# Turning the rotated q with VectorE squares and a buffer in HBM instead of with TensorE

## The chip, the core and the metric

One core of a Trainium2 chip runs the whole layer. The metric is the device time of one execution in microseconds (us), the median of several runs. Beside the runs there is one profiled execution: every engine's instructions with their times, the DMAs and the clock granted to TensorE.

## What is computed

The reference is one layer of a decoder trunk on 256 positions of width 1024: a SwiGLU feed-forward half-step, a mixer of two attentions, a second half-step and a final norm. The change lies in the mixer, in the first attention ("MoBA"):

```python
proj = u @ w_in
q_a, k_a, v_a, q_b, k_b, v_b, g_a, g_b = jnp.split(proj, cuts, axis=-1)
q_a = partial_rotary(split_heads(q_a, N_HEADS_MOBA), positions)
k_a = partial_rotary(split_heads(k_a, N_HEADS_MOBA), positions)
y_a = merge_heads(moba_attention(q_a, k_a, split_heads(v_a, N_HEADS_MOBA)))
```

There are 8 heads of 64. The rotation changes the first 16 numbers of each head's 64. With 256 positions there is one block of keys, so this attention is a causal softmax of q·k.

## The kernel before

Positions stand on the 128 partitions, in two halves t = 0 and 1. A matrix product takes tiles of 128 rows by 512 columns of weights. Each number is split into a high and a low part, so that one product of a tile is three matmuls (`mm3`, L290; one call of `unit`, L296, is one half with one tile).

**Weights.** `Weights` (L129) loads tiles in pairs: `raw74` is load 74 and holds the tiles 148 and 149. Three load buffers take turns, so that load n+3 waits until both tiles of load n have been read by VectorE. ScalarE casts the high part (`wh`, L163), VectorE the low one (`wl`, L164); ten buffers of each take turns, and `pump` runs up to seven tiles ahead of TensorE. Tiles 132 to 139 are those of q, 140 to 147 of k, 148 to 155 of v.

**Order.** TensorE and SyncE run what the program writes, in that order; in this stretch the other engines do too. Side work is put between the units by `Weave`: a piece of work is a generator, `tick` is called once for a unit, and `yield n` lets n units pass. The constants at the top (`D_TURN`, `D_LANDED` and so on) are such counts.

**Projection and heads.** `project` (L648) does the 16 units of one projection: all eight tiles of t = 0 and then those of t = 1 for q, t = 1 two tiles behind t = 0 after that. Results are taken out of three accumulator banks by ScalarE (`evac`, L678). `rotate` (L660) is four instructions on POOL. `turn` (L692) then brings q and k from positions on the partitions to heads on the partitions, which the scores need: here by eight TensorE transposes of 128x128 into two PSUM banks (`qtpa`, `ktpa`, L701). ScalarE casts the high part (`qTha`, L313) and VectorE makes the low part (`qTla`, L314), in two halves of 512 columns each. The second attention's q and k are not rotated and go another way: VectorE transposes squares of 32x32 (L689), and sixteen DMAs from SBUF to SBUF let the squares change places (`exchange`, L413).

**The use.** `moba_pair` (L765) makes the scores `S` of two heads, adds the mask, makes the softmax on ScalarE and VectorE, transposes it on TensorE (`ptp`, L794) and multiplies with v. The first pair starts when q and k are there.

Of the kernel before, what the change touches and what calls it, by code (L numbers as in the profile page):

```python
# [8 lines left out]
F32 = mybir.dt.float32  # L9
# [8 lines left out]
P = 128  # L18
# [19 lines left out]
D_TURNED = 3  # L38
# [3 lines left out]
D_PIECE = 2  # L42
D_TURN = 10
D_READY = 7
D_NORM = 4
D_SQUARES = 3
D_EIGHT = 6
# [141 lines left out]
def hybrid_layer_kernel(ctx, tc, x, xt, pos, g_final, bgate, wstream, out):  # L189
    nc = tc.nc  # L190
# [3 lines left out]
    ordered.enter_context(tc.manual_schedule())  # L194
    consts = ctx.enter_context(tc.tile_pool(name="consts", bufs=1))
    wpool = ctx.enter_context(tc.tile_pool(name="wpool", bufs=1))
    work = ctx.enter_context(tc.tile_pool(name="work", bufs=1))
    psum = ctx.enter_context(tc.tile_pool(name="psum", bufs=1, space=PSUM))

# [9 lines left out]
    def big(nm, dt=F32R):  # L209
        return work.tile([P, 1024], dt, name=nm, tag="big", bufs=24)  # L210
# [7 lines left out]
    def row512(nm):  # L218
        return work.tile([P, 512], F32, name=nm, tag="tok", bufs=4)
# [66 lines left out]
    weave = Weave()  # L286
# [30 lines left out]
    def square(t, ms, cols):  # L317
        junk = work.tile([P, D], BF16, name=f"sq_{ms.name}", tag="junk", bufs=1)
        nc.scalar.activation(junk[:, cols], h[t][:, cols], AF.Square, scale=1.0 / 32.0, accum_out=ms)
# [55 lines left out]
    class Given(Normed):  # L375
# [15 lines left out]
        def blk(self, k):  # L391
            o = k % 4 * T + self.t * P
            return [q[:, o:o + P] for q in self.made[k // 4 * 2:k // 4 * 2 + 2]]

    def lagged(n, lag):

        for k in range(n + lag):
            if k < n:
                yield 0, k
            if k >= lag:  # L400
                yield 1, k - lag
# [4 lines left out]
    def slots(q, n):  # L406

        return q[:, 0:n * P].rearrange("p (g s w) -> p s g w", g=4, s=n)

    def plain(q):  # L410
        return q.rearrange("p (s g w) -> p s g w", g=4, w=32)

    def exchange(moved, squares, n, queues, gap):  # L413

        w = 32
        for m in range(16):
            i, j = divmod(m, 4)
            queues[m % len(queues)].dma_start(moved[j * w:j * w + w, i * n * w:(i + 1) * n * w],
                                              squares[i * w:i * w + w, j * n * w:(j + 1) * n * w])
            if m % len(queues) == len(queues) - 1:  # L420
                yield gap


    def ffn(base, xn, nm, on_half, lag, last=False):

# [2 lines left out]
        squares = {}  # L428

        def hidden(b, t, bank):  # L430
# [10 lines left out]
            nc.vector.transpose(dst, plain(sh[:, 256:512]))  # L441
            if t == 1 and (b % 2 or b == FB - 1):
                weave.add(turn_hidden(p, n), D_TURNED)

        def later(f, *args):
            f(*args)
            return
            yield

        def turn_hidden(p, n):  # L450
            moved = big(f"hm_{nm}{p}", F32)
            yield from exchange(moved, squares[p], n, [nc.sync], D_MOVE)
            yield D_MOVED
            hts[p] = big(f"hth_{nm}{p}"), big(f"htl_{nm}{p}")
            split(plain(hts[p][0][:, 0:n * P]), plain(hts[p][1][:, 0:n * P]), slots(moved, n))

        for b in range(FB):
# [14 lines left out]
            for t, k in lagged(KD, 2 if b else lag) if b or lag else ():  # L472
                if k == 0:
                    banks[t] = acc_bank(f"gu_{nm}{b}_{t}")
                i = base + b * KD + k
# [53 lines left out]
        for t, c in ((0, 0), (0, 1), (1, 0), (1, 1)) if last else ((0, 0), (1, 0), (0, 1), (1, 1)):  # L529
            pieces = (0, 1) if last and (t, c) == (1, 1) else (None,)  # L530
            for piece in pieces:
                for k in range(head, KF):
                    i = base + 2 * head + c * tail + k - head
# [91 lines left out]
    def next_norm(dst, nm):  # L625
        def on_half(t, c, piece=None):
# [9 lines left out]
            else:  # L636
                weave.add(go(), D_NORM)

# [21 lines left out]
    def rotate(dst, t):  # L660

        d3 = dst.rearrange("p (h d) -> p h d", d=HD)
        t1 = work.tile([P, NH, 16], F32, name=f"t1_{dst.name}", tag="rot1", bufs=2)
        t2 = work.tile([P, NH, 16], F32, name=f"t2_{dst.name}", tag="rot2", bufs=2)
        g = nc.gpsimd
        g.tensor_mul(t1, d3[:, :, 0:16], cos[:, t, :].unsqueeze(1).to_broadcast([P, NH, 16]))
        g.tensor_mul(t2[:, :, 0:8], d3[:, :, 8:16], sin[:, t, 0:8].unsqueeze(1).to_broadcast([P, NH, 8]))
        g.tensor_mul(t2[:, :, 8:16], d3[:, :, 0:8], sin[:, t, 8:16].unsqueeze(1).to_broadcast([P, NH, 8]))
        marks["rot"] = g.tensor_add(d3[:, :, 0:16], t1, t2).ins

    def heads(b0, nm, res, rotary, diagonal):


        for j, which in enumerate("qk"):
            src = {}
            squares = None if rotary else big(f"{which}s{nm}", F32)

            def evac(t, ps, j=j, which=which, src=src, squares=squares):  # L678
                dst = row512(f"{which}{nm}{t}")
                if j == 0:  # L680
                    if nm == "a":
                        nc.gpsimd.tensor_scalar(rq[t], un[t].r, 0.125, None, op0=ALU.mult)
                    nc.scalar.activation(dst, ps, AF.Copy, scale=rq[t])
                else:
                    nc.scalar.activation(dst, ps, AF.Copy, scale=un[t].r)
                if rotary:
                    rotate(dst, t)
                else:
                    nc.vector.transpose(slots(squares, 8)[:, t:t + 7:2], plain(dst))  # L689
                src[t] = dst  # L690

            def turn(which=which, src=src, squares=squares):  # L692
                if rotary:
                    tp = two_banks(f"{which}tp{nm}")
                else:
                    tp = big(f"{which}m{nm}", F32)
                    yield from exchange(tp, squares, 8, [nc.sync, nc.gpsimd], 1)
                    yield D_LANDED
                for pr in range(4 if rotary else 0):
                    for t in range(2):  # L700
                        nc.tensor.transpose(tp[:, pr * 256 + t * P:pr * 256 + (t + 1) * P], src[t][:, pr * P:(pr + 1) * P], ident)  # L701
                if which != diagonal:
                    parts = big(f"{which}Th{nm}"), big(f"{which}Tl{nm}")
                    for c in range(2):
                        s = slice(c * 512, c * 512 + 512)
                        if rotary:
                            split(parts[0][:, s], parts[1][:, s], tp[:, s])
                        else:
                            split(plain(parts[0][:, s]), plain(parts[1][:, s]), slots(tp, 8)[:, c * 4:c * 4 + 4])
                            yield D_PIECE  # L710
                    ready = [[q[:, pr * 256:(pr + 1) * 256] for q in parts] for pr in range(4)]
                else:
                    tp4 = slots(tp, 8).rearrange("p (c t) g w -> p c t g w", t=2)
                    for c in range(2):
                        for j in range(2):
                            rows = slice(j * HD, j * HD + HD)
                            dst = [q[rows].rearrange("p (c j t g w) -> p c j t g w", c=2, j=2, t=2, g=4)[:, :, j] for q in res["bd"][c]]
                            split(dst[0], dst[1], tp4[rows, c * 2:c * 2 + 2])
                            yield D_PIECE
                    ready = [[q[:, pr % 2 * 512:pr % 2 * 512 + 512] for q in res["bd"][pr // 2]] for pr in range(4)]  # L720
                yield D_READY if rotary else D_READY - D_PIECE
                res[which] = ready

            if which == diagonal:
                res["bd"] = [(big(f"bdh{nm}{c}"), big(f"bdl{nm}{c}")) for c in range(2)]
                for c in range(2):
                    for q in res["bd"][c]:
                        for half in range(2):
                            q5 = q[half * HD:(half + 1) * HD].rearrange("p (c j t) -> p c j t", c=2, j=2)
                            nc.gpsimd.memset(q5[:, :, 1 - half, :].bitcast(F32), 0.0)  # L730
            project(b0 + j, evac)
            weave.add(turn(), D_TURN if rotary else D_TURNED)

        vs = big(f"vh{nm}"), big(f"vl{nm}")

        def evac_v(t, ps):
            s = slice(t * 512, t * 512 + 512)
            nc.scalar.activation(vs[0][:, s], ps, AF.Copy, scale=un[t].r)
            nc.vector.scalar_tensor_tensor(vs[1][:, s], ps, un[t].r, vs[0][:, s].bitcast(F32),
                                           op0=ALU.mult, op1=ALU.subtract)  # L740
            if t == 1:
                res["v"] = [[q[:, s * 512:(s + 1) * 512] for q in vs] for s in range(2)]

        project(b0 + 2, evac_v)
# [133 lines left out]
    for gi in range(4):  # L878
        bg = work.tile([P, 512], F32, name=f"bg{gi}", tag="bg", bufs=2)
        src = bgate[gi * 512:(gi + 1) * 512]  # L880
# [20 lines left out]
    for c in range(2):  # L901
        banks = {}
        for t, k in lagged(4, 2):
            if k == 0:
                banks[t] = acc_bank(f"ba{t}{c}")
            i = W_BR + c * 4 + k
# [28 lines left out]
    for t in range(2):  # L935
        for c in range(2):
            ps = acc_bank(f"bb{t}{c}")
            for k in range(4):
                i = W_BR + 8 + c * 4 + k
# [8 lines left out]
    for c in range(2):  # L948
        s = slice(c * 512, c * 512 + 512)
        for t in range(2):  # L950
            ps = acc_bank(f"wo{t}{c}")
            for k in range(KD):
                i = W_OUT + c * KD + k
# [101 lines left out]
```

## Time and profile before

| | |
|---|---|
| median of 3 runs | 556.45 us (556.43 to 556.68) |
| profiled execution, its own time | 555.9 us |
| its span | 554.2 us |
| TensorE | 99% busy, 2494 matmuls |
| VectorE, ScalarE, POOL | 72%, 61%, 13% busy |
| granted TensorE clock, mean | 0.997 of full speed |
| read from HBM, written to it | 102.25 MB, 1.05 MB |

The span runs from the first to the last instruction; the execution's own time is 1.7 us longer. A busy share is the time in which an engine had an instruction at work. In a timeline a row gives the start, the time it took, the engine, the line and operation, what is written and read, and in brackets the engine's idle time before it with what ended it. A row with x4 stands for four in sequence, from the start of the first to the end of the last. Matmuls overlap: one takes 0.39 us from start to end, and the next starts 0.23 us after it.

### The profile page before, as it was taken

The numbers are of one execution on the slowest core, as the hardware profiler recorded it, in microseconds if no ns is written. First come the engines' busy times: TensorE is split into PE (matmuls) and PEld (weight loads), VectorE is DVE, ScalarE is ACT, GpSimd is POOL, SyncE is SP. The second block draws the span as 40 slices with busy tenths as digits, with TensorE's granted clock in tenths as the row PEclk, the third lists the DMA queues.
The fourth block names the chain that finished last, engine by engine and source line by source line (L and its number), as shares of the span: only waits on it lengthen the run. The fifth ranks groups of instructions, "written<-read, shape, count | busy, mean of one in ns | idle before, by whom it ended". The sixth has DMA issues, their size and how long they took to land.

```text
span 554.2 us, 7853 instructions
## 1 busy us (share of the span) xinstructions
PE 546.1 (99%) x2494; PEld 449.5 (81%) x2494; DVE 401.3 (72%) x694; ACT 338.1 (61%) x576; POOL 70.1 (13%) x141
## 2 busy tenths in 40 slices
PE   9999999999999999999999999999999999999995
PEld 5788888888888888888888888888888888888884
DVE  6887788766466676889888888777677678655645
ACT  6865656655454767677875774476556566544633
POOL 1200000000003746022022200460000000000000
PEclk9999999999999999999999999999999999999998
DMA  8946766775685677455545464576657766757722
GB/s 311 403 141 202 220 216 216 220 237 184 210 235 179 200 232 220 155 159 183 176 151 172 137 202 149 179 242 216 219 180 234 238 206 200 229 179 230 243 79 76
DMA packets 42937, 111.69 MB, mean 202 GB/s; under 512 B 8080, under 2 KB 16528, under 8 KB 42896
## 3 DMA queue, kind: packets, MB, share of 16 engines
q1 hardware_dynamic: 40464, 107.90, 60.9%
q0 software_dynamic: 2000, 2.62, 1.8%
q10 hardware_dynamic: 432, 0.67, 0.3%
q8 instruction: 19, 0.31, 0.3%
q14 instruction: 22, 0.18, 0.1%
HBM read 102.25 MB, written 1.05 MB: 186 GB/s over the span
## 4 chain that ended last, share of the span: by engine, by line
PE 95%; DMA 3%; ACT 0%; DVE 0%; issue 0%; ACTq 0%
PE gu_f L293 14%; PE gu_f L294 14%; PE gu_f L292 14%; PE dn_f L294 7%; PE dn_f L292 7%; PE dn_f L293 7%; PE in L292 7%; PE in L294 7%; PE in L293 7%; DMA raw<-in_wstream 2%; PE wo L294 1%; PE wo L292 1%; PE wo L293 1%; PE y_a L748 1%; PE z L748 1%; PE y_b L748 1%
## 5 line engine op out<-in xcount | busy, mean ns | idle before, releaser
L164 DVE SCALAR_TENSOR_TENSOR wl<-raw,first,wh 128x512 fp32r<-128x512 f32 x256 | 181.8, 747 | 41.3 <-ACT wh L163 40.1
L163 ACT ACTIVATE wh<-raw,first 128x512 fp32r<-128x512 f32 x256 | 171.7, 717 | 56.3 <-DMA raw<-in_wstream 31.0
L160 ACT CAST wh<-raw 128x512 fp32r<-128x512 f32 x120 | 70.4, 620 | 63.9 <-DMA raw<-in_wstream 40.8
L161 DVE TENSOR_TENSOR wl<-raw,wh 128x512 fp32r<-128x512 f32 x120 | 78.6, 691 | 40.0 <-ACT wh L160 39.9
L292 PE MATMUL gu_f<-wh,zh 128*128 128x512 f32 x176 | 68.6, 390 | 0.0
L294 PE MATMUL gu_f<-wh,zl 128*128 128x512 f32 x176 | 68.5, 389 | 0.0
L293 PE MATMUL gu_f<-wl,zh 128*128 128x512 f32 x176 | 68.5, 389 | 0.0
L292 PE MATMUL dn_f<-wh,hth_f 128*128 128x512 f32 x172 | 67.1, 390 | 0.0
L294 PE MATMUL dn_f<-wh,htl_f 128*128 128x512 f32 x172 | 66.9, 389 | 0.0
L293 PE MATMUL dn_f<-wl,hth_f 128*128 128x512 f32 x172 | 66.9, 389 | 0.0
L292 PE MATMUL in<-wh,uh 128*128 128x512 f32 x160 | 63.5, 397 | 0.0
L293 PE MATMUL gu_f<-wl,xh 128*128 128x512 f32 x160 | 62.4, 390 | 0.3 <-DVE wl L164 0.3
L294 PE MATMUL in<-wh,ul 128*128 128x512 f32 x160 | 62.5, 391 | 0.0
L292 PE MATMUL gu_f<-wh,xh 128*128 128x512 f32 x160 | 62.4, 390 | 0.1
L293 PE MATMUL in<-wl,uh 128*128 128x512 f32 x160 | 62.4, 390 | 0.0
L294 PE MATMUL gu_f<-wh,xl 128*128 128x512 f32 x160 | 62.2, 389 | 0.0
L293 PEld LDWEIGHTS gu_f<-wl,zh 128*128 128x128 f32 x176 | 33.0, 188 | 6.9
L294 PEld LDWEIGHTS gu_f<-wh,zl 128*128 128x128 f32 x176 | 33.0, 188 | 6.8
L292 PEld LDWEIGHTS gu_f<-wh,zh 128*128 128x128 f32 x176 | 33.0, 188 | 6.8
L292 PEld LDWEIGHTS dn_f<-wh,hth_f 128*128 128x128 f32 x172 | 32.3, 188 | 6.9 <-DVE sh_f L433 0.4
L294 PEld LDWEIGHTS dn_f<-wh,htl_f 128*128 128x128 f32 x172 | 32.3, 188 | 6.7
L293 PEld LDWEIGHTS dn_f<-wl,hth_f 128*128 128x128 f32 x172 | 32.3, 188 | 6.7
(247 smaller groups left out, 756.5 us busy)
## 6 DMA issues: line engine op xcount, KB each, us to landing
raw<-in_wstream SPq DMA_DIRECT2D x184, 512.0 KB, 4.3
hm_f<-hs_f SPq DMA_DIRECT2D x160, 32.0 KB, 4.2
raw<-in_wstream SPq DMA_DIRECT2D x8, 256.0 KB, 4.9
h<-in_x SPq DMA_DIRECT2D x2, 512.0 KB, 6.6
bg<-in_bgate POOLq DMA_DIRECT2D x4, 256.0 KB, 4.6
xin<-in_xt SPq DMA_DIRECT2D x3, 256.0 KB, 5.1
hm_f<-hs_f SPq DMA_DIRECT2D x32, 16.0 KB, 3.1
gB<-in_g_final POOLq DMA_DIRECT2D x1, 512.0 KB, 6.2
```

Source lines behind the costliest of these rows:

```text
L160: self.nc.scalar.copy(hi, raw)
L161: self.nc.vector.tensor_sub(lo, raw, hi.bitcast(F32))
L163: self.nc.scalar.activation(hi, raw, AF.Copy, scale=g)
L164: self.nc.vector.scalar_tensor_tensor(lo, raw, g, hi.bitcast(F32), op0=ALU.mult, op1=ALU.subtract)
L292: nc.tensor.matmul(o, ah, wh, start=first, stop=False)
L293: nc.tensor.matmul(o, ah, wl, start=False, stop=False)
L294: nc.tensor.matmul(o, al, wh, start=False, stop=last)
L748: nc.tensor.matmul(o, a[p], b[q], start=first and i == 0, stop=last and i == 2, skip_group_check=True)
```

## The change

The q of the first attention is no longer turned by TensorE; k still is. After the rotation VectorE transposes squares of 32x32 (`square`), four units after each half's evacuation. SyncE writes the whole tile of squares to a buffer in HBM, `there`, and nine units later reads it back in four DMAs, each of which gathers what one group of 32 partitions wrote, so that squares change places (`by_hbm`). Six units after that the two parts are made as before, now from SBUF (`qma`). Two more large tiles are used (`qsa`, `qma`), and two PSUM banks less.

```diff
+D_WRITTEN = 9
+D_ROTATED = 4
+D_SQUARED = 3
...
+    hbm = ctx.enter_context(tc.tile_pool(name="hbm", bufs=1, space=bass.MemoryType.DRAM))
...
+    def by_hbm(moved, squares, n):
+        w = n * 32
+        there = hbm.tile([P, 4 * w], F32, name="there")
+        nc.sync.dma_start(there, squares)
+        yield D_WRITTEN
+        for i in range(4):
+            nc.sync.dma_start(moved[:, i * w:(i + 1) * w],
+                              there[i * 32:i * 32 + 32, :].rearrange("r (j c) -> j r c", j=4))
...
-            squares = None if rotary else big(f"{which}s{nm}", F32)
+            squares = None if rotary and j else big(f"{which}s{nm}", F32)
+
+            def square(t, src, squares=squares):
+                nc.vector.transpose(slots(squares, 8)[:, t:t + 7:2], plain(src))
...
                 if rotary:
                     rotate(dst, t)
+                    if j == 0:
+                        weave.add(later(square, t, dst), D_ROTATED)
                 else:
-                    nc.vector.transpose(slots(squares, 8)[:, t:t + 7:2], plain(dst))
+                    square(t, dst)
...
-                if rotary:
+                if squares is None:
                     tp = two_banks(f"{which}tp{nm}")
                 else:
                     tp = big(f"{which}m{nm}", F32)
-                    yield from exchange(tp, squares, 8, [nc.sync, nc.gpsimd], 1)
+                    if rotary:
+                        yield from by_hbm(tp, squares, 8)
+                    else:
+                        yield from exchange(tp, squares, 8, [nc.sync, nc.gpsimd], 1)
                     yield D_LANDED
-                for pr in range(4 if rotary else 0):
+                for pr in range(4 if squares is None else 0):
...
-            weave.add(turn(), D_TURN if rotary else D_TURNED)
+            weave.add(turn(), D_TURN if squares is None else D_ROTATED + D_SQUARED if rotary else D_TURNED)
```

On VectorE, behind the cast of tile 141, stood before the casts of the next weight tiles (`wl142` is tile 142, `raw71` its load):

```order
L164 SCALAR_TENSOR_TENSOR wl142_2094<-raw71_1987,first_73,wh142_2093 128x512
L164 SCALAR_TENSOR_TENSOR wl143_2101<-raw71_1987,first_73,wh143_2100 128x512
L164 SCALAR_TENSOR_TENSOR wl144_2110<-raw72_2026,first_73,wh144_2109 128x512
L164 SCALAR_TENSOR_TENSOR wl145_2117<-raw72_2026,first_73,wh145_2116 128x512
L164 SCALAR_TENSOR_TENSOR wl146_2145<-raw73_2054,first_73,wh146_2144 128x512
L164 SCALAR_TENSOR_TENSOR wl147_2152<-raw73_2054,first_73,wh147_2151 128x512
L164 SCALAR_TENSOR_TENSOR wl148_2161<-raw74_2104,first_73,wh148_2160 128x512
L164 SCALAR_TENSOR_TENSOR wl149_2172<-raw74_2104,first_73,wh149_2171 128x512
```

and now, at the same place:

```order
L694 STREAM_TRANSPOSE qsa_2013<-qa0_2080 128x4x4x32
L167 SCALAR_TENSOR_TENSOR wl142_2097<-raw71_1989,first_75,wh142_2096 128x512
L167 SCALAR_TENSOR_TENSOR wl143_2104<-raw71_1989,first_75,wh143_2103 128x512
L167 SCALAR_TENSOR_TENSOR wl144_2114<-raw72_2029,first_75,wh144_2113 128x512
L167 SCALAR_TENSOR_TENSOR wl145_2121<-raw72_2029,first_75,wh145_2120 128x512
L167 SCALAR_TENSOR_TENSOR wl146_2149<-raw73_2057,first_75,wh146_2148 128x512
L167 SCALAR_TENSOR_TENSOR wl147_2156<-raw73_2057,first_75,wh147_2155 128x512
L694 STREAM_TRANSPOSE qsa_2013<-qa1_2135 128x4x4x32
L167 SCALAR_TENSOR_TENSOR wl148_2165<-raw74_2107,first_75,wh148_2164 128x512
L167 SCALAR_TENSOR_TENSOR wl149_2177<-raw74_2107,first_75,wh149_2176 128x512
```

The two squares stand ahead of the casts of tiles 142 and 148.

SyncE's queue had only weight loads here. Now it reads:

```order
L152 DMA raw74_2107<-in_wstream 128x1024
L152 DMA raw75_2124<-in_wstream 128x1024
L152 DMA raw76_2159<-in_wstream 128x1024
L152 DMA raw77_2180<-in_wstream 128x1024
L437 DMA there_2189<-qsa_2013 128x1024
L152 DMA raw78_2205<-in_wstream 128x1024
L152 DMA raw79_2227<-in_wstream 128x1024
L440 DMA qma_2188<-there_2189 128x1x256 x4
L152 DMA raw80_2275<-in_wstream 128x1024
```

The write has got its place behind load 77, the four reads (x4) theirs behind load 79.

ScalarE cast q (L313) ahead of tile 154 before; now it does so behind tile 158:

```order
L166 ACTIVATE wh154_2264<-raw77_2180,first_75 128x512
L703 ACTIVATE ka0_2229<-in1_0_2144,r_u0_1833 128x512
L166 ACTIVATE wh155_2271<-raw77_2180,first_75 128x512
L166 ACTIVATE wh156_2280<-raw78_2205,first_75 128x512
L703 ACTIVATE ka1_2250<-in1_1_2168,r_u1_1884 128x512
L166 ACTIVATE wh157_2291<-raw78_2205,first_75 128x512
L166 ACTIVATE wh158_2307<-raw79_2227,first_75 128x512
L317 CAST qTha_2300<-qma_2188 128x512 x2
L166 ACTIVATE wh159_2319<-raw79_2227,first_75 128x512
L166 ACTIVATE wh160_2346<-raw80_2275,first_75 128x512
L166 ACTIVATE wh161_2356<-raw80_2275,first_75 128x512
L317 CAST kTha_2337<-ktpa_2328 128x512 x2
```

The two casts of q moved behind both evacuations of k (`ka0`, `ka1`), and three casts of weights stand between them and those of k. VectorE's `qTla` moved with them. On TensorE the eight rows of `qtpa` are gone; POOL's order is as it was.

## Rows read from the trace of the kernel before

**Rows 1.** Page, part 1: engine, busy us, share of the span, instructions.

```profile
PE 546.1 (99%) x2494; PEld 449.5 (81%) x2494; DVE 401.3 (72%) x694; ACT 338.1 (61%) x576; POOL 70.1 (13%) x141
```

**Rows 2.** Page, part 4: the chain that ended last, by engine.

```profile
PE 95%; DMA 3%; ACT 0%; DVE 0%; issue 0%; ACTq 0%
```

**Rows 3.** Timeline, 203 to 208.5 us: start, us, engine, line, operation.

```profile
204.43 0.40 PE L294 MATMUL in<-wh,ul 128*128 128x512 f32 x1
204.67 1.04 PE L701 MATMUL qtpa<-ident,qa 128*128 128x128 f32 x8
205.77 0.39 PE L293 MATMUL in<-wl,uh 128*128 128x512 f32 x1
207.85 0.39 PE L293 MATMUL in<-wl,uh 128*128 128x512 f32 x1
```

**Rows 4.** Timeline of PE before k's transposes, 214 to 220 us.

```profile
213.75 0.39 PE L292 MATMUL in<-wh,uh 128*128 128x512 f32 x1
216.24 0.39 PE L294 MATMUL in<-wh,ul 128*128 128x512 f32 x1
```

**Rows 5.** Groups by line and form: times, busy us, mean ns, idle before.

```profile
L689 DVE STREAM_TRANSPOSE qsb<-qb 128x512 f32<-128x512 f32 x2 | 1.4, 705 | 0.0
L313 ACT CAST kThb<-kmb 128x512 fp32r<-128x512 f32 x2 | 1.1, 618 | 0.0
```

**Rows 6.** Timeline of POOL: rotation of q, then k's second half.

```profile
194.23 0.90 POOL L666 TENSOR_TENSOR t_qa<-qa,cos 128x128 f32<-128x128 f32 x1
195.10 0.76 POOL L667 TENSOR_TENSOR t_qa<-qa,sin 128x64 f32<-128x64 f32 x1
196.67 0.79 POOL L669 TENSOR_TENSOR qa<-t_qa,t_qa 128x128 f32<-128x128 f32 x1
199.62 0.32 POOL L667 TENSOR_TENSOR t_qa<-qa,sin 128x64 f32<-128x64 f32 x1
...
211.28 0.46 POOL L666 TENSOR_TENSOR t_ka<-ka,cos 128x128 f32<-128x128 f32 x1
212.82 0.46 POOL L669 TENSOR_TENSOR ka<-t_ka,t_ka 128x128 f32<-128x128 f32 x1
```

**Rows 7.** Timeline of DVE, 192 to 200 us.

```profile
192.30 0.74 DVE L164 SCALAR_TENSOR_TENSOR wl<-raw,first,wh 128x512 fp32r<-128x512 f32 x1
194.06 3.08 DVE L164 SCALAR_TENSOR_TENSOR wl<-raw,first,wh 128x512 fp32r<-128x512 f32 x4 [1.02 <-ACT wh L163]
```

**Rows 8.** A weight load: its issue on SP; another's time to landing.

```profile
199.36 0.33 SPq L149 DMA_DIRECT2D raw<-in_wstream  x1
DMA to landing us min/median/max: 3.2/3.2/3.2
```

**Rows 9.** DMA issues: KB each, us to landing; first row 186-226 us.

```profile
raw<-in_wstream SPq DMA_DIRECT2D x15, 512.0 KB, 4.0
...
hm_f<-hs_f SPq DMA_DIRECT2D x160, 32.0 KB, 4.2
h<-in_x SPq DMA_DIRECT2D x2, 512.0 KB, 6.6
xin<-in_xt SPq DMA_DIRECT2D x1, 128.0 KB, 3.3
```

**Rows 10.** Timeline: two casts of weights; k's cast, p's last product, its transposes.

```profile
199.01 1.34 ACT L163 ACTIVATE wh<-raw,first 128x512 fp32r<-128x512 f32 x2
...
217.54 0.59 ACT L313 CAST kTha<-ktpa 128x512 fp32r<-128x512 f32 x1
...
229.11 0.48 DVE L790 TENSOR_SCALAR p<-p,st 128x128 f32<-128x128 f32 x2
...
231.38 0.82 PE L794 MATMUL ptp<-ident,p 128*128 128x128 f32 x6
```

**Rows 11.** Timeline of PE: third tile of k; where v's second half begins.

```profile
199.45 0.39 PE L293 MATMUL in<-wl,uh 128*128 128x512 f32 x1
...
211.71 0.39 PE L292 MATMUL in<-wh,uh 128*128 128x512 f32 x1
```

More of the change, by code (lines that the diff above doesn't have):

```diff
@@ L393, in blk, with later @@
             return [q[:, o:o + P] for q in self.made[k // 4 * 2:k // 4 * 2 + 2]]
+    def later(f, *args):
+        f(*args)
+        return
+        yield
     def lagged(n, lag):
@@ L443, in hidden @@
                 weave.add(turn_hidden(p, n), D_TURNED)
[L445 to L448, printed above, removed]
         def turn_hidden(p, n):
@@ L675, in heads, with evac @@
             src = {}
-            squares = None if rotary else big(f"{which}s{nm}", F32)
-            def evac(t, ps, j=j, which=which, src=src, squares=squares):
+            squares = None if rotary and j else big(f"{which}s{nm}", F32)
+            def square(t, src, squares=squares):
+                nc.vector.transpose(slots(squares, 8)[:, t:t + 7:2], plain(src))
+            def evac(t, ps, j=j, which=which, src=src, square=square):
                 dst = row512(f"{which}{nm}{t}")
@@ L705, in turn @@
                         s = slice(c * 512, c * 512 + 512)
-                        if rotary:
+                        if squares is None:
                             split(parts[0][:, s], parts[1][:, s], tp[:, s])
@@ L720, in turn @@
                     ready = [[q[:, pr % 2 * 512:pr % 2 * 512 + 512] for q in res["bd"][pr // 2]] for pr in range(4)]
-                yield D_READY if rotary else D_READY - D_PIECE
+                yield D_READY if squares is None else D_READY - D_PIECE
                 res[which] = ready
```

## The prediction

> **What bounds the kernel.** I read the page first. TensorE is busy for 99% of the span [rows 1], and the chain that ended last runs 95% over TensorE [rows 2]: time that TensorE is spared, or loses, reaches the end one for one, and work on the other engines costs nothing until TensorE waits for it. So I read the stretch from 190 to 232 us in order of time: the eight transposes of q, from 204.67, in the stream of projection matmuls [rows 3], the same matmuls undisturbed [rows 4], then who feeds TensorE here. Those are the weight casts (ScalarE `wh`, VectorE `wl`), the loads behind them, and the way of q and k to the scores.
>
> **What is removed.** The last matmul ahead of q's transposes starts at 204.43, the second behind them at 205.77: 1.34 us [rows 3]. Undisturbed, 11 steps take 216.24 - 213.75 = 2.49 us, 0.226 each [rows 4]; two steps would be 0.45. The transposes cost 0.89. The nine steps from 205.77 to 207.85 take 2.08 where 2.04 is usual [rows 3, 4]: 0.04 more. Together **0.93 us**, 0.17% of the time. Nothing stands between them and the end but TensorE's own stream, so all of it is gained if no wait takes its place.
>
> **What is added, busy time.** Two squares on VectorE at 0.705 us, by the ones that turn q of the other attention [rows 5]: 1.4 us. ScalarE's two casts of q read a square-ordered SBUF tile instead of PSUM; the like cast of k takes 0.618 [rows 5], about the 0.59 of a cast from PSUM [rows 10]. SyncE issues five DMAs more, 0.33 us each by the row of a weight load [rows 8], and 1 MB more is moved. All of it costs nothing as busy time: VectorE has 28% and ScalarE 39% of the span free [rows 1]. What could cost is the order, since both engines and SyncE's queue work strictly in theirs.
>
> **The wait that is added on VectorE.** The first square stands right behind the cast that began at 192.30 [rows 7], and it needs the rotated q. POOL rotates it from 194.23 and ends at 196.67 + 0.79 = 197.46 [rows 6]. Before, VectorE made four casts in that time, from 194.06 on, 3.08 us [rows 7]; now it stands still and they come after the square. Does the rotation end sooner when VectorE is idle? The rotation of k's second half took from 211.28 to 212.82 + 0.46, 2.0 us [rows 6]; so the end lies between 194.23 + 2.0 = 196.23 and 197.46. I take the middle, 196.85, since single steps took both lengths (L667: 0.76 and 0.32) [rows 6].
>
> The Trainium skill (SBUF — State Buffer, Who interferes with whom) says that a VectorE instruction with two SBUF inputs contends with a GpSimd instruction that reads SBUF; by it the early end, 196.23, would hold, since VectorE then runs nothing. The trace agrees only in part: the 0.76 ran beside casts and the 0.32 nearly without, but the 0.79 at 196.67 outlasted the last of the four casts, which ended at 197.14.
>
> From 196.85: square 0.705, 197.55; two casts, half of 3.08, 199.1. Only then is the buffer free into which load raw74 goes; it lands 3.2 us later by the landing of the load in this place [rows 8], 202.3; two ScalarE casts take 1.34 [rows 10], VectorE's last 0.74 [rows 7]: 204.4. Now raw77 is issued, and right behind it, 0.33 later [rows 8], the write to HBM: **204.7**. With the early rotation it is 204.1; with the late one and a landing of 4.0 [rows 9] it is 206.1.
>
> Does TensorE feel this delay of some 3 us? The first of the four casts ends about 197.55 + 0.75 = 198.3, and its tile, the third of k's projection, is first multiplied at 199.45 [rows 11]: covered. Next is k's first evacuation, which stands behind raw77's first cast on ScalarE. Landing 204.4 + 4.0 [rows 9], cast and evacuation 0.67 each (half of 1.34): 209.74. TensorE wants the bank for the second half of v at 211.71 [rows 11], now 0.93 sooner, 210.78. A margin of 1.0; with the late end, 205.8 + 4.0 + 1.34 = 211.14, TensorE loses 0.4.
>
> **The way through HBM.** The trace has no write to HBM of this size in this stretch. Its nearest rows: a load of the same 512 KB lands in 3.2 us alone [rows 8] and in 6.6 where it stands behind others, as the two of h do at the start [rows 9]. The write starts right behind raw77, so not alone, but behind one load only: I take the middle, 4.9. The reads wait on SyncE for the landing; the fourth is issued 3 x 0.33 = 1.0 later, and 128 KB takes 3.3 (the part of x) to 4.2 (moves with the same rows of 1 KB) [rows 9]. I take 4.2, for the rows' length. The trip is 4.9 + 1.0 + 4.2 = **10.1 us**; its ends are 3.2 + 1.0 + 3.3 = 7.5 and 6.6 + 1.0 + 4.2 = 11.8. While SyncE waits for the write, load raw80 queues behind the reads; its buffer, raw77's, is freed by casts that follow the landing at 208.4, so hardly before the reads go out at 204.7 + 4.9 = 209.6.
>
> How long may it take? ScalarE casts q ahead of three weight casts and of k's two casts. Before, k's first cast began at 217.54, the softmax's last product of the first pair ended at 229.11 + 0.48 = 229.59, and TensorE transposed it at 231.38 [rows 10], now 230.45: the chain may slip by 0.86, k's cast to 218.40. Ahead of it go two casts of q (1.2) and three of weights (2.0, at half of 1.34): q must have landed by **215.2**. From 204.7 that leaves 10.5 us, 0.4 more than the trip; with the ends of the issue, 11.1 or 9.1. Each microsecond over it costs TensorE one.
>
> Costed at nothing: two more of the 24 large tiles shift which old tile a later one replaces; POOL's clearing of the next q's tiles may wait for TensorE there. Cover: those tiles are first filled when the next q has been moved, after 230 us.
>
> **Sum.** The profiled execution took 555.9 us (span 554.2); less 0.93 it is 554.97. The median of the runs lies 0.55 above it, so I forecast 556.45 - 0.93 = **555.5 us**, with q's new way just hidden.
>
> **Rivals.**
> *Slower: the trip outlasts its cover.* The place is ScalarE's cast of q, behind which weight casts and k queue. From 10.5 us on (9.1 at worst) it costs one for one: the gain is gone at 11.4, and 0.2% is lost from 12.5. Worst ends together, 11.8 - 9.1 = 2.7 lost, give 556.45 - 0.93 + 2.7 = 558.2. For it: a margin of only 0.4, and three loads of 512 KB crowd around the trip. Against it: the loads here land in 4.0 at the median, near the short end.
> The Trainium skill (VectorE: DVE Perf Modes, Rules for kernel authors) names TensorE for a transpose of 128x128 if it may end in PSUM, which speaks against this change; it gives no price for squares with a detour, so the sum stays by the rows.
> *Partly given back:* the same wait, up to 2 us lost, or k's late evacuation (0.4): 555.7 to 557.5. A typical time is 556.2.
> *Faster by more than 0.93:* a stop of the weight stream costs more than the cadence shows, which would need 1.11. 555.2. Against it: the same matmuls are back at 0.23 within two steps [rows 3].
> That the change does not do what it says is excluded for TensorE: the order has eight transposes fewer there and is otherwise the same.
>
> **Numbers.** What a measurement of this kernel can tell from no change is about 0.2%, 1.11 us. Hidden (555.5): 0.52. Partly given back: 0.27, within 0.2% of before. Slower: 0.14. Faster: 0.07. So 0.07, 0.79, 0.14. The range 555.1 to 557.4 holds the first case, nearly all of the second and some of the last.
>
> **What would show it.** Right: no TensorE transposes of q, matmul starts unbroken to k's transposes, the first square ending at 197 to 198.2, the HBM write issued at 204 to 206, q's cast on ScalarE beginning before 215.2, and the first transposes of the softmax near 230.5. Wrong: ScalarE idle on the reads past 215.5 and TensorE idle at the scores or at those transposes; TensorE idle at the second half of v or at k's transposes, if the late casts decide; a write that needs over 7 us.

## The result and the profile after

The changed kernel takes 563.17 us (median of 4 runs, 562.13 to 564.21), the kernel before on the same chip 556.50: a ratio of 1.0119, interval 1.0100 to 1.0139. It is 6.7 us slower where 0.93 less was forecast, and outside the range. The profiled execution took 562.96 us, its span is 561.2 us against 554.2.

Page of the changed kernel, part 1 (answers [rows 1]) and part 4, the chain by engine (answers [rows 2]):

```profile
PE 548.8 (98%) x2486; PEld 449.6 (80%) x2486; DVE 401.6 (72%) x696; ACT 337.5 (60%) x576; POOL 68.5 (12%) x141
...
PE 84%; DVE 6%; DMA 6%; ACT 2%; issue 1%; SPq 0%; ACTq 0%; DVEq 0%
```

Eight matmuls are gone, yet TensorE is busy 2.7 us longer, and its share of the chain fell from 95% to 84%. VectorE stands on the chain now, and DMAs with 6% instead of 3%. Timeline of TensorE, at the places of [rows 3], [rows 11] and [rows 10]; the first two rows stand where q's transposes stood between them:

```profile
205.10 0.39 PE L298 MATMUL in<-wh,ul 128*128 128x512 f32 x1
205.32 0.39 PE L296 MATMUL in<-wh,uh 128*128 128x512 f32 x1
...
211.44 0.45 PE L296 MATMUL in<-wh,uh 128*128 128x512 f32 x1
...
225.03 0.38 PE L799 MATMUL S<-kTha,qTha 64*128 64x256 f32 x2 [2.89 <-ACT kTha L317]
226.11 0.39 PE L799 MATMUL S<-kTla,qTha 64*128 64x256 f32 x2 [0.70 <-DVE kTla L318]
...
236.74 0.85 PE L817 MATMUL ptp<-ident,p 128*128 128x128 f32 x6
```

The transposes of q are out and the starts run on at 0.23 us. The matmul that was at 204.43 is now at 205.10. That is 0.67 later, as TensorE has been since the first loads. The first matmul of v's second half moved from 211.71 to 211.44, so 0.93 is gained in between. Then TensorE waits 2.89 and 0.70 us for k's parts at the scores, and the softmax's transposes start 5.36 us later than before, at 236.74.

The chain of waits through that stretch (start, us, what):

```profile
202.81 1.38 DVE wl L167 x2
204.21 0.33 SPq L152
204.59 6.62 DMA there<-qsa
211.22 0.67 SPq L440
...
213.10 8.40 DMA qma<-there
221.52 0.63 ACT qTha L317
222.18 1.18 DVE qTla L318 x2
223.39 2.07 DVE wl L167 x3
225.46 0.61 DVE kTla L318
...
236.31 0.48 DVE p L813 x2
```

The write takes 6.62 us, the last read 8.40. SyncE needs 1.9 us from the first of the four issues to the last (211.22 to 213.10). From 204.59 to 221.52 the trip is 16.9 us long where the prediction took 10.1 and counted 10.5 as covered. ScalarE stands still for the reads, and behind q queue the weight casts and k:

```profile
221.52 1.14 ACT L317 CAST qTha<-qma 128x512 fp32r<-128x512 f32 x2 [6.43 <-DMA qma<-there]
222.57 1.94 ACT L166 ACTIVATE wh<-raw,first 128x512 fp32r<-128x512 f32 x3
224.42 0.56 ACT L317 CAST kTha<-ktpa 128x512 fp32r<-128x512 f32 x1
```

Engines by stretch, with the heading of the view (PEclk is the granted clock as a share of full speed, "DMA share" that of the 16 DMA engines' time):

```profile
core 0: us, PE busy (x) PEld busy (x) DVE busy (x) ACT busy (x) POOL busy (x), PEclk, DMA share, GB/s
205.00:222.00 17.00, 17.00 (x80) 13.73 (x78) 6.57 (x9) 6.98 (x12) 9.54 (x18) 1.00 0.82 234
222.00:226.60 4.60, 1.01 (x11) 0.67 (x12) 3.88 (x6) 3.49 (x8) 0.00 (x0) 1.00 0.43 161
226.60:230.00 3.40, 3.40 (x15) 2.71 (x12) 3.29 (x6) 3.40 (x7) 0.00 (x0) 0.50 0.53 166
240.00:275.00 35.00, 34.85 (x179) 27.47 (x177) 32.06 (x62) 26.34 (x62) 7.91 (x16) 1.00 0.55 172
```

After the two waits the granted clock is 0.50, 1.2 GHz, for 3.4 us. Matmul by matmul against before, TensorE is 0.26 us ahead at 211, 3.89 behind when the projection goes on at 226.95, 5.30 behind at 230 (the slow clock), 5.36 at the softmax's transposes and 6.8 from 275 on. By this trace the slow clock was not what decided: the last product of the softmax ends at 236.31 + 0.48 = 236.79, as TensorE gets to it, so a faster TensorE would have waited there. No run tried that apart. The last 1.4 us go in pieces of up to 0.4 between 257 and 269 us of the profile before (262 to 276 here). The chain that ended last runs over VectorE and ScalarE there, and VectorE, busy for 32.06 us of 35, has little room to catch up.

### The profile page after: what moved, and what is told of

It is laid out like the page before. It is cut to its first block, busy times and chain, and to the rows that moved or that the text cites. A ratio compares the mean times of both kernels' runs of the same rounds, so it can differ in the third digit from the quotient of the medians.

```text
span 561.2 us, 7837 instructions
## 1 busy us (share of the span) xinstructions
PE 548.8 (98%) x2486; PEld 449.6 (80%) x2486; DVE 401.6 (72%) x696; ACT 337.5 (60%) x576; POOL 68.5 (12%) x141
## 4 chain that ended last, share of the span: by engine, by line
PE 84%; DVE 6%; DMA 6%; ACT 2%; issue 1%; SPq 0%; ACTq 0%; DVEq 0%
PE gu_f L297 14%; PE gu_f L298 13%; PE gu_f L296 13%; PE dn_f L297 7%; PE dn_f L296 7%; PE dn_f L298 7%; PE in L296 4%; PE in L298 4%; PE in L297 4%; DMA raw<-in_wstream 2%; DVE wl L167 2%; DMA qma<-there 1%; PE wo L296 1%; PE wo L298 1%; PE wo L297 1%; DMA there<-qsa 1%
```

## The experiments

Two theories stood at the start. **Four engines:** each of the four reads has a source whose outermost dimension is 4, and only 4 of the 16 DMA engines carry it, the same 4 each time. **Just written or short rows:** data in rows of 1 KB, or just written, comes back slowly beside weight loads, in whatever shape.

| run | squares | way of q | median us | ratio to before (interval) |
|---|---|---|---|---|
| the change | early | 4 reads, outermost 4 | 563.17 | 1.0119 (1.0100 to 1.0139) |
| e1_16_reads | early | 16 reads of 32 rows | 561.12 | 1.0084 (1.0069 to 1.0099) |
| e2_8_reads | early | 8 reads, outermost 2 | 567.62 | 1.0203 (1.0185 to 1.0220) |
| e6_dead_trip | early | TensorE; the change's trip unused | 562.57 | 1.0110 (1.0097 to 1.0123) |
| e4_no_trip | early | none | 556.95 | 1.0009 (0.9998 to 1.0020) |
| e8_no_trip_late_squares | late | none | 555.46 | 0.9982 (0.9973 to 0.9991) |
| e10_late_squares | late | 4 reads, outermost 4 | 560.71 | 1.0084 (1.0067 to 1.0101) |
| e3_spread_trip | early | 4 writes, 1 read, spread | 556.74 | 0.9999 (0.9990 to 1.0008) |
| e9_spread_late | late | 4 writes, 1 read, spread | 555.52 | 0.9985 (0.9977 to 0.9994) |
| e11_same_reads | late | 4 writes, 4 reads, outermost 128 | 555.42 | 0.9983 (0.9973 to 0.9992) |
| e5_exchange_late | late | 16 moves from SBUF to SBUF | 556.10 | 0.9994 (0.9985 to 1.0003) |

The kernel before took 556.35 or 556.36 beside these. TensorE and SyncE have the same order in all but for the DMAs named; a scheduler sets that of ScalarE and VectorE by its own estimates, so where q's way changes, q's and k's casts can move past one or two weight casts.

**The shape of the reads: 16 DMAs, and 8.**

```diff
-        for i in range(4):
-            nc.sync.dma_start(moved[:, i * w:(i + 1) * w],
-                              there[i * 32:i * 32 + 32, :].rearrange("r (j c) -> j r c", j=4))
+        for m in range(16):
+            i, j = divmod(m, 4)
+            nc.sync.dma_start(moved[j * 32:j * 32 + 32, i * w:(i + 1) * w],
+                              there[i * 32:i * 32 + 32, j * w:(j + 1) * w])
```

> The same 512 KB come back from HBM in the same rows of 1 KB, but in 16 DMAs of 32 rows each instead of 4 DMAs whose source has an outermost dimension of 4. Theory A (each of the four reads ran on 4 of the 16 DMA engines, the same four, so they stood in line): the rows are now spread over all engines, the last read lands about 4 us after its issue instead of 8.4, q is there at 216 to 217 instead of 221.5, and the time falls to 556.5 to 558. Theory B (rows that were just written come back slowly, or rows of 1 KB are slow beside the weight loads): nothing of that changes, the last read still lands 8 us after its issue, and the time stays at 563.

Measured: 561.12, between the theories' numbers. Each read now lands fast, in 2.1 us at the median, but sixteen issues keep SyncE until 218.00. The tile `qma` in this run, and then SyncE's timeline:

```profile
DMA to landing us min/median/max: 1.7/2.1/4.3
```

```profile
210.70 7.30 SPq L441 DMA_DIRECT2D qma<-there  x16
218.10 0.84 SPq L152 DMA_DIRECT2D raw<-in_wstream  x2
```

So q was there no sooner (its cast began at 221.64), and load 80 was issued at 218.10 instead of 213.72. Rows of 1 KB that were just written are not slow; the expectation of both theories forgot the issues.

Eight reads in place of the four:

```diff
...
+        for m in range(8):
+            i, j = divmod(m, 2)
+            nc.sync.dma_start(moved[j * 64:j * 64 + 64, i * w:(i + 1) * w],
+                              there[i * 32:i * 32 + 32, j * 2 * w:(j + 1) * 2 * w].rearrange("r (j c) -> j r c", j=2))
```

> The same bytes and rows come back in 8 DMAs whose source has an outermost dimension of 2. Theory A (as many DMA engines as that dimension says): each read runs on 2 engines with 32 rows on each, so eight of them stand in line instead of four; the last lands 16 to 18 us after its issue, q is there at 229 to 231, and the time rises to 570 to 573. Theory B (just written, or short rows beside loads): bytes and rows are the same, so 563 as with the change.

Measured: 567.62; the last read lands at 227.5, 16.7 us after the first issue where the change needed 10.3. Same bytes, same rows: the outermost dimension decides. The time is 2.4 us short of what theory A said: q came 1.5 us sooner, and the pieces behind 257 us are not lost here. How many engines work is in the trace: the share of the 16 engines' time while only these reads move (packets, MB, share), in this run (214 to 216 us, outermost 2),

```profile
q1 hardware_dynamic: 94, 0.09, 13.6%
```

and with outermost 4, in e10_late_squares (211.8 to 212.8 us):

```profile
q1 hardware_dynamic: 99, 0.10, 27.8%
```

2 of 16 are 12.5%, 4 of 16 are 25%. The trace does not name the engines; that all four reads stand on the same four is read from the share, which stays near a quarter with all four under way. The Trainium skill (DMA: Bandwidth & Descriptors, Why a DMA increments its semaphore by 16 and not by 1) says that a DMA runs on the largest number of engines, up to 16, that divides the outermost dimension of both sides; the trace agrees with 2 and with 4, and a run below with 128. The prediction had not weighed this rule, which speaks against the change as written.

**Is the wait for q all of the loss?**

```diff
...
-            weave.add(turn(), D_TURN if squares is None else D_ROTATED + D_SQUARED if rotary else D_TURNED)
+            weave.add(turn(), D_TURN if rotary else D_TURNED)
+            if rotary and j == 0:
+                weave.add(by_hbm(big(f"{which}m{nm}", F32), squares, 8), D_ROTATED + D_SQUARED)
```

> q is turned by TensorE as before; squares, write and reads are all made at the places of the change, and nobody uses what they bring. Nothing is left out. Theory: the loss is the wait for q alone, so this takes 556.3 to 556.9, the time of before. Rival: the trip's traffic delays the weight loads behind it (load 80 landed at 222.9 with the change and at 213.6 before), and TensorE waits for their tiles: 558 or more, TensorE idle from 226 on.

Measured: 562.57; the theory fell and the rival holds, though not at its place. With nobody waiting for q the loss is nearly the same: 6.2 us, where the change lost 6.7 and the 0.93 that it had gained. Load 80 stands behind the reads on the four engines. In the changed kernel, between the landing of the last read (221.52) and that of load 80 (222.88), what is left of the loads and the gates' DMAs uses 27% of the 16 engines' time, or about four engines (221.6 to 222.8 us):

```profile
q1 hardware_dynamic: 20, 0.07, 13.8%
q0 software_dynamic: 16, 0.06, 13.1%
```

DMA issues of 212.5 to 213 us (KB each, us to landing) in the run with the unused trip, and then ScalarE's timeline:

```profile
raw<-in_wstream SPq DMA_DIRECT2D x1, 512.0 KB, 8.9
```

```profile
221.76 1.34 ACT L166 ACTIVATE wh<-raw,first 128x512 fp32r<-128x512 f32 x2 [6.54 <-DMA raw<-in_wstream]
223.01 0.56 ACT L317 CAST kTha<-ktpa 128x512 fp32r<-128x512 f32 x1
```

That load, 80, takes 8.9 us (3.3 in the kernel before); ScalarE waits 6.54 us for it, and k's cast queues behind. TensorE loses at the scores first, not at load 80's own tiles. Either of two things, q or load 80, would have made k late.

**VectorE's wait for POOL.** The squares' own price: no write, no reads, q cast from the squares as they stand.

```diff
...
-                        yield from by_hbm(tp, squares, 8)
+                        tp = squares
+                        yield D_WRITTEN
```

> Squares, VectorE's wait for POOL and the late weight casts as in the change, but no write and no reads: q is cast from the squares where they stand, so blocks of q are left in the wrong place and the scores are those of another q. Theory: all that was lost is the trip, and the rest of the change is hidden; then the removed transposes are gained in full, 0.8 to 0.95 us: 555.5 to 555.8. Rival: VectorE's wait for POOL and the loads that it delays cost TensorE something too; then 556.2 or more, with TensorE idle at the second half of v or at k's transposes.

Measured: 556.95, not distinguishable from before, so by the medians 1.5 us are lost without any trip, more than the gain: the rival. The 12 runs spread from 555.38 to 558.55, the kernel before from 555.87 to 556.86, so some runs lose nothing and some 3 us; the profiled execution, 558.14, is one of the slow ones. In it TensorE loses 1.2 us at a place that neither had named, the softmax's transposes, and another 1.5 between 257 and 269 us of the profile before, where the change lost its last 1.4. Timelines of ScalarE and of TensorE in this run:

```profile
223.84 0.72 ACT L166 ACTIVATE wh<-raw,first 128x512 fp32r<-128x512 f32 x1 [3.15 <-DMA raw<-in_wstream]
```

```profile
232.03 0.85 PE L818 MATMUL ptp<-ident,p 128*128 128x128 f32 x6 [1.07 <-DVE p L814]
```

What ScalarE waits for is load 82. It meets two DMAs of the gates' bias, which POOL issues behind k's rotation. The DMA issues of 215 to 215.5 us in this run:

```profile
bg<-in_bgate POOLq DMA_DIRECT2D x2, 256.0 KB, 8.3
raw<-in_wstream SPq DMA_DIRECT2D x1, 512.0 KB, 8.6
```

In the kernel before, load 82 took 4.7 us. Then the squares alone were moved (the change's lines on top of the run above):

```diff
...
-                nc.vector.transpose(slots(squares, 8)[:, t:t + 7:2], plain(src))
+                with tc.issue_after(W.low[(AFTER0, AFTER1)[t]]) if rotary else ExitStack():
+                    nc.vector.transpose(slots(squares, 8)[:, t:t + 7:2], plain(src))
...
-                        weave.add(later(square, t, dst), D_ROTATED)
+                        weave.add(later(square, t, dst), D_ROTATED + (3 if t else 5))
```

`W.low` holds the low cast of each tile; `AFTER0, AFTER1 = 145, 149`.

> As the run without write and reads (q is again cast from the squares where they stand, so the scores are those of another q), but the squares stand later on VectorE: the first behind the cast of tile 145 instead of 141, the second behind 149 instead of 147, when POOL has finished. Theory: the 1.5 us that the run without the trip fell short of the removed transposes come from VectorE's wait for POOL, which makes loads 74 to 79 some 2.5 us late until they meet the gate loads of POOL; without the wait the loads are issued as before and the gain is whole: 555.3 to 555.7, and load 82 lands at 220 to 221 instead of 223.7. Rival: the shortfall has nothing to do with the wait (two VectorE instructions more, other tiles of SBUF); then 556.7 to 557.2 again.

Measured: 555.46, the theory. The transposes start at 230.99 with no wait, nothing is lost behind 257 us, and load 82, issued within 0.1 us of the run before, lands at 219.75 instead of 223.74; the gates' DMAs go out at 212.41 instead of 214.55. That shows the wait as the cause; that it works through the meeting of load 82 with the gates' DMAs is read from the two traces and was not tried apart. The same move with the change's trip:

> The change with only the two squares moved on VectorE, behind the casts of tiles 145 and 149; write and reads as in the change. Theory of two causes: VectorE's wait is gone, so loads 74 to 79 go out as before; the write is issued at 203 to 204 and the last of the four reads lands 8 us after its issue, at 217 to 219, and load 80 behind it as late; 558 to 560.5, between the change and before. Rival (VectorE's wait is the whole cause): 555.5 to 556. Rival (the trip is the whole cause): 562 or more.

Measured: 560.71, the theory of two causes, 0.2 above its range: the write goes out at 203.33, the last read lands 8.5 us after its issue, at 218.90, load 80 takes 9.8.

**The reads spread over all engines.**

```diff
-        nc.sync.dma_start(there, squares)
+        for i in range(4):
+            nc.sync.dma_start(there.rearrange("(j r) (i c) -> i r j c", j=4, i=4)[i],
+                              squares[i * 32:i * 32 + 32, :].rearrange("r (j c) -> r j c", j=4))
...
-        for i in range(4):
-            nc.sync.dma_start(moved[:, i * w:(i + 1) * w],
-                              there[i * 32:i * 32 + 32, :].rearrange("r (j c) -> j r c", j=4))
+        nc.sync.dma_start(moved, there)
```

> Squares where the change has them; the squares change places in the write (four DMAs of 32 rows each, every row in 4 pieces of 1 KB), and one read of 128 rows of 4 KB brings all back. Both have an outermost dimension that 16 divides. Theory (reads on 4 of the 16 DMA engines delay q and the loads behind them): the write lands in 5 to 6.5 us, the read in about 4.5, q is there at 215 to 216, load 80 lands within 5 us; what stays is VectorE's wait: 556.5 to 558. Rival (any 1 MB of traffic at this place delays the loads): load 80 takes 8 us or more again, and the time is 560 or more.

Measured: 556.74, the theory: 6.4 us of the loss are gone with the shape of the DMAs alone. What stays is the early squares' price, again not the same in every run (555.25 to 557.34). In the profiled execution, 556.76, load 82 lands late once more, at 223.81, yet TensorE waits neither at the scores nor at the softmax's transposes: all of the loss, 1.5 us, falls between 257 and 269 us of the profile before. What holds TensorE there no run tried apart.

The same with late squares:

> Both mended: squares behind the casts of tiles 145 and 149, write in four DMAs that swap the places, one read. Nothing is left out. Theory of two causes: q is there by 214 to 215, load 80 lands within 5 us of its issue, and the removed transposes are gained: 555.3 to 556.0. Rival (a third cause, such as the traffic as such or the longer queue of SyncE): 557 or more.

Measured: 555.52, the gain that was forecast. VectorE, the tile `qma` and TensorE in this run:

```profile
198.17 0.71 DVE L696 STREAM_TRANSPOSE qsa<-qa 128x512 f32<-128x512 f32 x1 [0.35 <-POOL qa L685]
...
202.44 0.71 DVE L696 STREAM_TRANSPOSE qsa<-qa 128x512 f32<-128x512 f32 x1 [0.35 <-POOL qa L685]
```

```profile
DMA to landing us min/median/max: 4.6/4.6/4.6
```

```profile
222.00 0.38 PE L801 MATMUL S<-kTha,qTha 64*128 64x256 f32 x2
```

No wait is left at the scores. One thing still differed from the change's reads: their number and the length of their rows. With the same write, but `there[:, i * w:(i + 1) * w]` read in four DMAs:

> Late squares and the write that swaps places, as in the run with both mended, but the way back is four reads of 128 KB with rows of 1 KB again, as many and as large as in the change; only their outermost dimension is 128 (rows) and not 4 (groups). Theory (the outermost dimension of 4 holds a read on 4 DMA engines): each read lands 3.5 to 5 us after its issue, q is there before 215, and the time is that of the run with both mended, 555.3 to 556.0. Rival (four reads with rows of 1 KB are slow beside the loads, whatever their shape): the last lands 8 us after its issue, as in the run with late squares alone, and the time is 560 to 561.

Measured: 555.42. Four reads of 128 KB with rows of 1 KB land in 5.4 to 5.7 us beside weight loads. The packets of one microsecond in this run (211 to 212 us), and of the one in e10_late_squares shown above (211.8 to 212.8 us):

```profile
DMA packets 251, 0.27 MB, mean 272 GB/s; under 512 B 27, under 2 KB 237, under 8 KB 251
```

```profile
DMA packets 99, 0.10 MB, mean 98 GB/s; under 512 B 3, under 2 KB 99, under 8 KB 99
```

The rows of 1 KB are those under 2 KB less those under 512 B: 210 with an outermost dimension of 128, though weight loads moved beside them, and 96 with 4. So it is the outermost dimension, and not the rows or their number. The landing is above the 3.5 to 5 expected, but q is there at 214.1.

**Without HBM.** Late squares, and `exchange` for both attentions:

```diff
-                    if rotary:
-                        yield from by_hbm(tp, squares, 8)
-                    else:
-                        yield from exchange(tp, squares, 8, [nc.sync, nc.gpsimd], 1)
+                    yield from exchange(tp, squares, 8, [nc.sync, nc.gpsimd], 1)
```

> Late squares, and q goes the way of the other attention's q: sixteen DMAs of 32 KB from SBUF to SBUF, on SyncE's and POOL's queues in turn, no HBM. Theory: one hop of about 4 us instead of two, all 16 DMA engines each time; q is there by 211 and the transposes are gained, 555.3 to 556.0, no better than the mended trip, since q had time until 215. Rival: eight more issues on SyncE at 0.42 to 0.46 us (as the 16 reads showed) delay loads 78 to 80 by up to 3.5 us, as VectorE's wait did: 556.7 or more.

Measured: 556.10, between the two; not distinguishable from before. q lands at 212.2, loads 78 and 79 go out 1 to 1.4 us later than before. Its profiled run has no wait behind 205 us that would explain the 0.6 to 0.7 us to the two best versions; that stays open. The spread trip with late squares is faster than both kernels in either form: by 0.15% and 0.17% than before, by 1.3% than the change.

## Why the prediction was wrong

- **The gain.** 0.93 us from eight transposes [rows 3, 4]: right, 0.93 in the profile, 0.84 to 0.94 as medians once nothing takes it back.
- **The square's wait on VectorE.** POOL was to end at 196.85, between 196.23 and 197.46 [rows 6]; it ended at 196.46 in a profile that runs 0.67 late, 195.79 in the time of the one before, so ahead of both ends. The whole rotation took 1.56 us with VectorE idle, where the early end had 2.0. The rule of the Trainium skill that the prediction had weighed (SBUF — State Buffer, Who interferes with whom) gave the early end. The trace agrees, with 1.56 us here and 3.2 beside the four casts [rows 6, 7]; the middle that was taken was 1.06 too late. That the write was issued at 204.59, within 0.1 us of the 204.7 forecast, is luck: in the time before it is 203.92, 0.8 early. Timelines of POOL and VectorE after:

```profile
196.00 0.46 POOL L684 TENSOR_TENSOR qa<-t_qa,t_qa 128x128 f32<-128x128 f32 x1
```

```profile
196.50 0.71 DVE L694 STREAM_TRANSPOSE qsa<-qa 128x512 f32<-128x512 f32 x1 [2.79 <-POOL qa L684]
```

- **"Does TensorE feel this delay?"** Wrong in its scope. The third tile and v's second half were covered, as it said. It stopped there: k's rotation, the gates' DMAs behind it on POOL (issued at 216.26, at 213.23 before) and load 82 were not followed. By the medians, early squares cost 1.5 us with no trip and 1.2 with a spread one, at the softmax's transposes and behind 257 us.
- **The way through HBM: this step failed.** The write took 6.6, its upper end, where 4.9 was taken, and the fourth read was issued 1.9 after the first, where 1.0 was taken. The reads were priced at 4.2, "for the rows' length", by moves of 32 rows [rows 9]; the last took 8.4, beyond both ends, because the price hangs on the shape of the DMA, which none of those rows shares. (The same write with late squares took 5.2, in e10_late_squares.)
- **The rival.** "The trip outlasts its cover", at the place named and one for one: q was to land by 215.2, which is 215.87 in a profile that runs 0.67 late, and it landed at 221.52, 5.65 after that. Its own rule then gives 556.45 - 0.93 + 5.65 = 561.2; measured 563.17. In the profile, 5.6 are lost up to the softmax's transposes (5.36 behind, 0.93 gained, less the 0.67 since the first loads), and 1.4 behind 257 us, which the rule left out. The rival had a chance of 0.14 and a bound of 558.2, both set by the read's price.
- **Load 80.** The prediction saw only its issue behind the reads. Its landing on the same four engines took 9.2 us. That alone, with the early squares, costs 6.2 us, as the unused trip shows; 3.4 of them are lost up to the softmax's transposes (3.84 behind, less 0.48 since the first loads), where the change lost 5.6. Without q's wait the change would still have taken some 561.6 us, an estimate from that run less the 0.93.

## What to carry to other kernels

Price a DMA by a row of the same shape, not of the same bytes: here an outermost dimension of 4 made four reads take 10.3 us from the first issue to the last landing, where 128 took 6.8, and held up the weight load behind them. When a load's way is to be swapped in blocks, put the swap on the side where the rows can stay outermost. An engine that waits in order passes its delay on to everything that is issued behind it, POOL's DMAs too; follow it to the end of the chain, and put the instruction behind the work that is ready.

## What the runs showed of the hardware

- Reads whose source had an outermost dimension of 2 or 4 used 13.6% and 27.8% of the 16 DMA engines' time while nothing else moved; with 4, 96 rows of 1 KB moved in a microsecond, with 128 it was 210 beside weight loads. A load of 512 KB that was issued behind reads with 4 landed in 8.9 to 9.8 us instead of 3.3.
- Waits of 2.89 and 0.70 us at the scores were followed by 3.4 us at 1.2 GHz. In e2_8_reads TensorE stood still from 222 to 230.8 and then went on; the granted clock was 0.50, 1.2 GHz, from 224.2 to 237.9.
